# Cross-attention of a two-layer decoder step: sample score rows four a step behind a head's maximum, weight parts behind the samples' part of the output, and the first query chunk finished ahead of the second

## The chip, the cores and the metric

The kernel runs on one core of a Trainium2 chip. The metric is the device time of one execution in microseconds (us). Each engine (TensorE or PE, VectorE or DVE, ScalarE or ACT, GpSimd or POOL, SyncE or SP) works through its own list of instructions in order; semaphores make one wait for another. DMA queues move data between the chip's memory and the on-chip buffers.

## The reference

One inference step of a decoder trunk of two layers, for a prompt of 256 tokens and for 8 samples of one token each. Both use the same weights, d_model is 1024, and all is fp32.

```python
def trunk(x, conv_state, rec_state, mem_k, mem_v):
    for i in range(2):
        x = x + 0.5 * swiglu(rmsnorm(x, norm_ffn1[i]), w_ffn1_gate[i], w_ffn1_up[i], w_ffn1_down[i])
        x = x + mixer_i(rmsnorm(x, norm_mix[i]))          # short conv (i = 0), gated recurrence (i = 1)
        x = x + cross_attn(rmsnorm(x, norm_xattn[i]), mem_k[i], mem_v[i], w_xq[i], w_xo[i])
        x = x + 0.5 * swiglu(rmsnorm(x, norm_ffn2[i]), w_ffn2_gate[i], w_ffn2_up[i], w_ffn2_down[i])
    return rmsnorm(x, norm_final)

def cross_attn(x, mk, mv, w_q, w_o):                       # 4 heads of 256, 256 memory positions
    q = (x @ w_q).reshape(B, T, 4, 256)
    p = softmax(einsum('bthd,bnhd->bhtn', q, mk) / 16)
    return einsum('bhtn,bnhd->bthd', p, mv).reshape(B, T, 1024) @ w_o
```

The prompt's memory keys and values are computed here, from `rmsnorm(mem) @ w_xkv`, and returned. The samples' keys and values come from two caches of (2 layers, 8 samples, 256 positions, 4 heads, 256): 16 MB a layer that have to be read.

## The kernel before

Activations stand transposed: 128 partitions, 8 slices of the model dimension, 264 columns (256 of the prompt, 8 of the samples). An fp32 product is three products in a reduced format (`mm3`): high part of the weights by high part of x, high by low, low by high. The program's names end in h and l for such parts.

**Weights** come in pieces of 512 KB through one stream (class `Weights`). SP issues the transfer into `raw`, ACT makes the high part `wh` (L110), and DVE or POOL makes the low part `wl` (L125), which is `raw` minus `wh`. `raw` has 6 buffers, the parts 5. In attention `W.lo` gives `wl` to POOL; once both pairs of heads are done for the samples, it gives it back to DVE. `W.after["v"]` holds an instruction, and each later `wl` on DVE is ordered behind it.

**The order of work.** TensorE's program is the spine. `flow.tick()` in it steps each "lane" of generators once, and every generator goes on to its next `yield`: so a generator's instructions come to stand between TensorE's products. A scheduler then lists each engine's instructions by their place in the program; `tc.high_priority` moves some forward, and `order(a, b)` says that `a` stands behind `b` on their engine.

**Attention of a layer** (`attention`): four query chunks, one per head. Chunks 0 and 1 share a pass: the first three slices of the one, the first three of the other, then slice by slice in turn (`project`). Chunks 2 and 3 follow. Then, for each head, the memory's keys and values (`do_kv`, tiles `kv`, 8 slices of 6 products). Then the output projection (`pj`).

Lane 1 holds the prompt: after `do_kv(h)` it transposes the keys (`pkt`), multiplies them by the queries (`psc`, L1070), takes the softmax (DVE maximum `mxp` L1057, ACT exponentials `Pp`, DVE reciprocal `zsp` L1060, ACT scale L1062), transposes the weights (`ppt`, L1084; split into `PTh` on ACT and `PTl` on DVE) and multiplies the values (`po`; result split into `oh` on ACT and `ol` on DVE).

Lane 0 holds the samples. Their scores use no TensorE products: the 256 positions of the 8 samples stand as 16 rows of 128 partitions, and DVE multiplies and sums one row an instruction (L1043, tile `junk`, 16 rows a head). `pq` brings a head's queries into that form. The key cache comes in `ring` tiles of 1 MB (8 rows; two a head, called 2a and 2b for head 2 here); there are four ring tiles, and a tile of head 2 can be fetched only once one of head 0 has been used. After a head's rows stand its maximum `mxs` and ACT's exponential. `sample_rest` follows: `SLACK` steps of pause, then the values of heads 0 and 1 (pair 0) and of heads 2 and 3 (pair 1), 64 DVE instructions `acc` a pair (L1153, L1156; the last two write `total`). Value tiles use the same ring. With the first pair goes `combine`, which joins the maxima and sums over the partitions through three small TensorE steps (`pst`, L1112, L1119, L1129); the first reads `mxs` of all heads. Behind each pair `spt` (L1173, TensorE) contracts `total`, and ACT and DVE split it into the samples' columns of `oh` and `ol` (L1180, L1181).

Of the kernel before, what the change touches and what calls it, by code (L numbers as in the profile page):

```python
# [8 lines left out]
F32 = mybir.dt.float32  # L9
# [4 lines left out]
AX = mybir.AxisListType  # L14
# [4 lines left out]
KT = D // P  # L19
T = 256  # L20
NB = 8
NC = T + NB
# [3 lines left out]
XH = 4  # L26
# [12 lines left out]
RING = 4  # L39
HURRY = 40  # L40
STAGGER = 3
SLACK = 5
STEPS = (3, 5, 7, 9, 11, 13)
LAG = 2
DOWN = ((0, 8), (8, 15), (15, 22))
# [199 lines left out]
def trunk_step(ctx: ExitStack, tc: tile.TileContext, ins, consts, outs, stop=None):  # L245
    nc = tc.nc
# [8 lines left out]
    def mm_bank(name):  # L255
        return pmm.tile([P, 512], F32, tag="mm", name=name)

    def aux_bank(name):
        return paux.tile([P, 512], F32, tag="aux", name=name)

    W = Weights(nc, wp)
    flow = Flow(W)
# [22 lines left out]
    xh = cp.tile([P, KT, NC], F32R, name="xh")  # L285
    xl = cp.tile([P, KT, NC], F32R, name="xl")
# [10 lines left out]
    def order(ins, first, reason):  # L297
        info = mybir.DependencyInfo(mybir.DependencyClass.NoSync, mybir.DependencyReason.DATA)
        tc.add_manual_dep(ins.ins, first.name, info, reason=reason)
# [14 lines left out]
    def act(dst, src, func, **kw):  # L314
        in_line(nc.scalar.activation(dst, src, func, **kw))  # L315
# [21 lines left out]
    def mm3(ps, w, rh, rl, first, last, s=slice(None)):  # L337
        wh, wl = w
        nc.tensor.matmul(ps, wh[:, s], rh, start=first, stop=False)  # L339
        nc.tensor.matmul(ps, wh[:, s], rl, start=False, stop=False)  # L340
        return nc.tensor.matmul(ps, wl[:, s], rh, start=False, stop=last).ins  # L341
# [66 lines left out]
            if not self.done:  # L408
                flow.drain(2)

    def project(nch, rh, rl, evac, kt_major=2, need=None, before=None, late_lo=False):
        if not callable(rh):
            rh, rl = (lambda k, t=rh: t[:, k]), (lambda k, t=rl: t[:, k])
        done = 0
        if kt_major:
            ws = [W.get() for _ in range(kt_major)]
            pss = [(c, j, mm_bank(f"pj{c}_{j}")) for c in range(kt_major) for j in range(2)]
            if late_lo:
                for first in (True, False):
                    for c in range(kt_major):  # L420
                        for r in (rh, rl) if first else (rh,):
                            for k in range(KT):
                                w = ws[c](k)[0 if first else 1]
                                for j in range(2):
                                    flow.passed = nc.tensor.matmul(
                                        pss[2 * c + j][2][:, :NC],
                                        w[:, j * P : j * P + P],
                                        r(k),
                                        start=first and k == 0 and r is rh,
                                        stop=not first and k == KT - 1,  # L430
                                    ).ins
                                if k % 4 == 3 and (first or k < KT - 1 or c < kt_major - 1):
                                    flow.tick()
            else:
                order = [(c, k) for c in range(kt_major) for k in range(STAGGER)]
                order += [(c, k) for k in range(STAGGER, KT) for c in range(kt_major)]
                for n, (c, k) in enumerate(order):
                    if before is not None and c == 0:
                        before(k)
                    for j in range(2):  # L440
                        s = slice(j * P, j * P + P)
                        mm3(pss[2 * c + j][2][:, :NC], ws[c](k), rh(k), rl(k), k == 0, k == KT - 1, s)
                    if n % kt_major == kt_major - 1:
                        if k == HK - 1:
                            W.release_first_halves(kt_major)
                        if n < len(order) - 1:
                            flow.tick()
            W.release()
            if need is not None:
                need.ready()  # L450
            with tc.high_priority(offset=HURRY):
                for c, j, ps in pss:
                    evac(c, j, ps[:, :NC])
            flow.tick()
            done = kt_major
        for c in range(done, nch):
            w = W.get()
            for j in range(2):
                ps = mm_bank(f"pj{c}_{j}")
                for k in range(KT):  # L460
                    mm3(ps[:, :NC], w(k), rh(k), rl(k), k == 0, k == KT - 1, slice(j * P, j * P + P))
                    if k == KT // 2 - 1:
                        flow.tick()
                if j == 1:
                    W.release()
                with tc.high_priority(offset=HURRY):
                    evac(c, j, ps[:, :NC])
                flow.tick()
# [342 lines left out]
    def ffn(norm, nxt):  # L811
        with tc.tile_pool(name="ff", bufs=1) as fp:
# [6 lines left out]
            def evac(c, j, ps):  # L819
# [12 lines left out]
                nc.gpsimd.tensor_sub(al[:, blk], a, ah[:, blk].bitcast(F32))  # L832

            project(FB, xh, xl, evac, need=norm, late_lo=norm.first)
            use_set(LNEXP)
            W.lo = ("p", "v", "v")
# [107 lines left out]
    def attention(l, norm, nxt):  # L944
        with tc.tile_pool(name="at", bufs=1) as ap:
# [4 lines left out]
            ol = ap.tile([P, KT, NC], F32R, name="ol")  # L950
            sc = ap.tile([P, XH, NI], F32, name="sc")
            oz = ap.tile([P, XH, NB], F32, name="oz")
            sampled = set()
            mx, zs, rz = (ap.tile([P, XH], F32, name=n) for n in ("mxs", "zss", "rzs"))
            tops = ap.tile([P, P], F32, name="tops")
            nc.gpsimd.memset(tops, 0.0)
# [68 lines left out]
            def spread(t):  # L1025

                return t.unsqueeze(len(t.shape)).broadcast_to(list(t.shape) + [P // NB])

            def sample_scores(h):

                zq = ap.tile([P, 2, P], F32, tag="zq", name="zq", bufs=1)
                nc.scalar.copy(zq.rearrange("p t (b g) -> p t b g", b=NB), spread(qTs[h][:, :, T:]))
                yield
                if h == 0:
                    yield
                pq = aux_bank("pq")
                for dt in range(2):
                    nc.tensor.transpose(pq[:, dt * P : dt * P + P], zq[:, dt], ident)
                yield
                for i in range(NI):  # L1040
                    t = ring.tiles[l, "k", h, i // 8].rearrange("p (i d) -> p i d", d=XD)
                    junk = ap.tile([P, XD], F32, tag="junk", name="junk", bufs=1)
                    nc.vector.tensor_tensor_reduce(  # L1043
                        junk, t[:, i % 8], pq[:, :XD], 1.0, 0.0, ALU.mult, ALU.add, sc[:, h, i : i + 1]
                    )
                    if i % 8 == 7:
                        ring.done((l, "k", h, i // 8))
                    if i % 5 == 4:
                        yield
                nc.vector.reduce_max(mx[:, h : h + 1], sc[:, h], axis=AX.X, negate=True)  # L1050
                act(sc[:, h], sc[:, h], AF.Exp, bias=mx[:, h : h + 1], accum_out=zs[:, h : h + 1])

            def softmax(src, npart, rows, name):
                pr = ap.tile([npart, rows, NMEM], F32, tag=f"P{name}", name=f"P{name}", bufs=1)
                mx = ap.tile([npart, rows], F32, tag=f"mx{name}", name=f"mx{name}", bufs=2)
                zs = ap.tile([npart, rows], F32, tag=f"zs{name}", name=f"zs{name}", bufs=2)
                nc.vector.reduce_max(mx, src, axis=AX.X, negate=True)  # L1057
                for r in range(rows):
                    act(pr[:, r], src[:, r], AF.Exp, bias=mx[:, r : r + 1], accum_out=zs[:, r : r + 1])
                nc.vector.reciprocal(zs, zs)  # L1060
                for r in range(rows):
                    nc.scalar.activation(pr[:, r], pr[:, r], AF.Copy, scale=zs[:, r : r + 1])  # L1062
                return pr
# [76 lines left out]
            def sample_rest():  # L1140

                for _ in range(SLACK):
                    yield
                steps = combine()
                for pair in range(XH // 2):
# [31 lines left out]
                    with tc.high_priority(offset=HURRY):  # L1177
                        ptv = pt[:, : 4 * NB].rearrange("p (t b) -> p t b", b=NB)
                        ohv, olv = (t[:, 4 * pair : 4 * pair + 4, T:] for t in (oh, ol))
                        nc.scalar.copy(ohv, ptv)  # L1180
                        nc.vector.tensor_sub(olv, ptv, ohv.bitcast(F32))  # L1181
                    sampled.add(pair)
                    yield

# [4 lines left out]
                    W.lo = ("v",)  # L1189

            flow.spawn(1, mem_split())
            project(XH, xh, xl, evac_q, need=norm)
            for h in range(XH):
                do_kv(h)
            out_proj(oh, ol, nxt, late=(KT - 2, lambda k: until(k // 4), lambda: flow.drain(1)))
# [490 lines left out]
```

## Time and profile before

| what | value |
|---|---|
| time, median of 3 runs (lowest, highest) | 1282.48 us (1280.98, 1283.21) |
| time of the profiled execution | 1282.15 us |
| its span in the trace | 1280.4 us |
| mean granted TensorE clock | 0.997 |
| TensorE busy | 1258.7 us, 98% of the span |
| DVE / ACT / POOL busy | 66% / 55% / 27% |
| attention of layer 0, with its output projection | about 300 to 419 us |
| attention of layer 1, the same | about 959 to 1075 us |

A row of the timeline gives start and duration in us, engine, line, operation, output and inputs, the count where rows are joined (x8), and in brackets the idle time of the engine before it with what ended it. A row of the waits gives the waiting engine and line, what it waited for, the total in us, the number of times, and the longest. A row of the windows gives a stretch, its length, then busy time (and instructions) of PE, PE's weight loads, DVE, ACT, POOL, the granted clock of TensorE (1.00 is full), the mean share of the DMA engines, and GB/s.

### The profile page before, as it was taken

The numbers are of one execution on the slowest core, as the hardware profiler recorded it, in microseconds if no ns is written. First come the engines' busy times: TensorE is split into PE (matmuls) and PEld (weight loads), VectorE is DVE, ScalarE is ACT, GpSimd is POOL, SyncE is SP. The second block draws the span as 40 slices with busy tenths as digits, with TensorE's granted clock in tenths as the row PEclk, the third lists the DMA queues.
The fourth block names the chain that finished last, engine by engine and source line by source line (L and its number), as shares of the span: only waits on it lengthen the run. The fifth ranks groups of instructions, "written<-read, shape, count | busy, mean of one in ns | idle before, by whom it ended". The sixth has DMA issues, their size and how long they took to land.

```text
span 1280.4 us, 25535 instructions
## 1 busy us (share of the span) xinstructions
PE 1258.7 (98%) x10039; PEld 1230.7 (96%) x10039; DVE 842.4 (66%) x1625; ACT 703.4 (55%) x1167; POOL 346.9 (27%) x272
## 2 busy tenths in 40 slices
PE   8999999999999999999999999999999999999996
PEld 8999999999789999999999999999999789999996
DVE  7655567758777655546655535887887787766454
ACT  6455544446655645544555544656566666766542
POOL 2211231214864211132111132000016862112220
PEclk9999999999999999999999999999999999999999
DMA  8795556655899666556666556653545997997550
GB/s 274 246 305 177 167 180 190 187 160 178 295 395 318 193 176 189 172 168 191 193 173 191 171 171 190 193 171 122 189 151 172 385 384 248 287 324 227 162 165 35
DMA packets 269898, 270.96 MB, mean 212 GB/s; under 512 B 8777, under 2 KB 259721, under 8 KB 269266
## 3 DMA queue, kind: packets, MB, share of 16 engines
q1 hardware_dynamic: 263870, 263.98, 65.4%
q10 hardware_dynamic: 5908, 5.35, 1.2%
q8 instruction: 79, 1.29, 0.4%
q14 instruction: 41, 0.34, 0.1%
HBM read 259.19 MB, written 10.10 MB: 210 GB/s over the span
## 4 chain that ended last, share of the span: by engine, by line
PE 91%; DVE 3%; ACT 2%; DMA 2%; POOL 1%; issue 1%; SPq 0%; DVEq 0%; POOLq 0%; ACTq 0%
PE pj L340 20%; PE pj L339 20%; PE pj L341 20%; PE dn L339 7%; PE dn L341 7%; PE dn L340 7%; PE kv L987 2%; PE kv L988 2%; PE kv L989 2%; ACT wh L110 1%; DVE wl L125 1%; PE pl L1333 1%; PE psc L1070 1%; DMA ring<-in_cache_mem_k_dram 1%; DVE xl L365 1%; DMA raw<-in_w_xkv_dram 1%
## 5 line engine op out<-in xcount | busy, mean ns | idle before, releaser
L125 DVE TENSOR_TENSOR wl<-raw,wh 128x1024 fp32r<-128x1024 f32 (+1 forms) x334 | 411.7, 1238 | 240.0 <-ACT wh L110 224.2
L339 PE MATMUL pj<-xh,wh 128*128 128x264 f32 x1952 | 557.8, 286 | 0.3 <-DVE g L824 0.3
L340 PE MATMUL pj<-xl,wh 128*128 128x264 f32 x1952 | 553.4, 284 | 0.0
L341 PE MATMUL pj<-xh,wl 128*128 128x264 f32 x1952 | 553.0, 283 | 0.0
L110 ACT CAST wh<-raw 128x1024 fp32r<-128x1024 f32 (+1 forms) x406 | 415.5, 1032 | 215.9 <-PE pj L340 107.8
L339 PEld LDWEIGHTS pj<-xh,wh 128*128 128x128 f32 x1952 | 367.7, 188 | 1.9 <-issue 1.4
L340 PEld LDWEIGHTS pj<-xl,wh 128*128 128x128 f32 x1952 | 368.0, 189 | 0.2
L341 PEld LDWEIGHTS pj<-xh,wl 128*128 128x128 f32 x1952 | 366.1, 188 | 0.0
L125 POOL TENSOR_TENSOR wl<-raw,wh 128x1024 fp32r<-128x1024 f32 (+1 forms) x74 | 173.3, 2356 | 127.2 <-ACT wh L110 108.3
L832 POOL TENSOR_TENSOR al<-a,ah 128x264 fp32r<-128x264 f32 x88 | 90.4, 1029 | 411.2 <-ACT ah L831 411.1
L339 PE MATMUL dn<-ah,wh 128*128 128x264 f32 x704 | 200.9, 285 | 0.0
L341 PE MATMUL dn<-ah,wl 128*128 128x264 f32 x704 | 200.0, 284 | 0.0
L340 PE MATMUL dn<-al,wh 128*128 128x264 f32 x704 | 199.4, 283 | 0.0
L341 PEld LDWEIGHTS dn<-ah,wl 128*128 128x128 f32 x704 | 132.7, 188 | 0.0
L339 PEld LDWEIGHTS dn<-ah,wh 128*128 128x128 f32 x704 | 132.4, 188 | 0.2
L340 PEld LDWEIGHTS dn<-al,wh 128*128 128x128 f32 x704 | 132.5, 188 | 0.0
L315 ACT ACTIVATE g<-g 128x264 f32<-128x264 f32 x88 | 36.9, 424 | 76.6 <-DVE g L824 76.6
L831 ACT CAST ah<-a 128x264 fp32r<-128x264 f32 x88 | 36.0, 413 | 68.2 <-DVE a L830 68.1
L360 ACT ACTIVATE xh<-xT,gains 128x264 fp32r<-128x264 f32 x56 | 28.1, 512 | 72.0 <-DVE xT L858 59.1
L1043 DVE CUSTOM_DVE_ANT_0 junk<-ring,pq 128x256 f32<-128x256 f32 x128 | 53.7, 420 | 12.3 <-DMA ring<-in_cache_mem_k_dram 8.6
L378 POOL TENSOR_TENSOR nacc_norm_xattn<-nacc_norm_xattn,nsq 128x264 f32<-128x264 f32 x14 | 13.6, 972 | 174.8 <-ACT nsq L377 174.5
L1156 DVE SCALAR_TENSOR_TENSOR acc<-ring,sc,acc 128x256 f32<-128x256 f32 x112 | 54.5, 487 | 2.7
(327 smaller groups left out, 1538.7 us busy)
## 6 DMA issues: line engine op xcount, KB each, us to landing
raw<-in_w_ffn_gate_dram SPq DMA_DIRECT2D x88, 512.0 KB, 5.8
raw<-in_w_ffn_up_dram SPq DMA_DIRECT2D x88, 512.0 KB, 4.6
raw<-in_w_ffn_down_dram SPq DMA_DIRECT2D x64, 512.0 KB, 4.1
ring<-in_cache_mem_k_dram SPq DMA_DIRECT2D x16, 1024.0 KB, 8.8
raw<-in_w_xkv_dram SPq DMA_DIRECT2D x64, 256.0 KB, 3.6
ring<-in_cache_mem_v_dram SPq DMA_DIRECT2D x16, 1024.0 KB, 9.1
raw<-in_w_rec_in_dram SPq DMA_DIRECT2D x32, 512.0 KB, 4.3
raw<-in_w_ffn_down_dram SPq DMA_DIRECT2D x32, 384.0 KB, 3.0
```

Of the source, the lines that this page charges most:

```text
L110: ins = self.behind(self.hi[i % len(self.hi)], copy(wh[:, :n], self.raw[i][:, :n]))
L125: ins = eng.tensor_sub(wl[:, :n], self.raw.pop(i)[:, :n], wh[:, :n].bitcast(F32))
L315: in_line(nc.scalar.activation(dst, src, func, **kw))
L339: nc.tensor.matmul(ps, wh[:, s], rh, start=first, stop=False)
L340: nc.tensor.matmul(ps, wh[:, s], rl, start=False, stop=False)
L341: return nc.tensor.matmul(ps, wl[:, s], rh, start=False, stop=last).ins
L360: W.pin(nc.scalar.activation(xh[:, k, :n], src, AF.Copy, scale=gcol(self.name, self.layer, k)))
L831: nc.scalar.copy(ah[:, blk], a)
L832: nc.gpsimd.tensor_sub(al[:, blk], a, ah[:, blk].bitcast(F32))
L987: nc.tensor.matmul(pss[nt], mh[:, k, t], wh, start=k == 0, stop=False)
L1043: nc.vector.tensor_tensor_reduce(junk, t[:, i % 8], pq[:, :XD], 1.0, 0.0, ALU.mult, ALU.add, sc[:, h, i : i + 1])
L1156: nc.vector.scalar_tensor_tensor(dst, t[:, i % 4, j], p, sums, op0=ALU.mult, op1=ALU.add)
```

## The change

Five edits, all in attention, in both layers:

1. A score row generator yields after every 4 rows instead of every 5, so a head takes one step more; `SLACK` goes from 5 to 1, so the samples' values begin at the same step.
2. Each score row is ordered behind the latest prompt maximum `mxp` that the program has made before it (`ahead`).
3. `wl` on DVE is ordered behind the samples' `ol`, the last DVE instruction of a pair (`W.after["v"]`).
4. `project` keeps its last product in `flow.passed`, behind which the small products of the samples are ordered.
5. Query chunks 0 and 1 take slices 3 and 4 in turn; then chunk 0 takes its slices 5 to 7 and is evacuated into `qT`, and only then chunk 1 takes its own.

```diff
-SLACK = 5
+SLACK = 1
...
-    def project(nch, rh, rl, evac, kt_major=2, need=None, before=None, late_lo=False):
+    def project(nch, rh, rl, evac, kt_major=2, need=None, before=None, late_lo=False, split=KT):
...
+        def out(c):
+            if need is not None:
+                need.ready()
+            with tc.high_priority(offset=HURRY):
+                for j in range(2):
+                    evac(c, j, pss[2 * c + j][2][:, :NC])
...
-                order += [(c, k) for k in range(STAGGER, KT) for c in range(kt_major)]
+                order += [(c, k) for k in range(STAGGER, split) for c in range(kt_major)]
+                order += [(c, k) for c in range(kt_major) for k in range(split, KT)]
...
-                        mm3(pss[2 * c + j][2][:, :NC], ws[c](k), rh(k), rl(k), k == 0, k == KT - 1, s)
+                        flow.passed = mm3(
+                            pss[2 * c + j][2][:, :NC], ws[c](k), rh(k), rl(k), k == 0, k == KT - 1, s
+                        )
+                    if split < KT and k == KT - 1:
+                        out(c)
...
-            if need is not None:
-                need.ready()
-            with tc.high_priority(offset=HURRY):
-                for c, j, ps in pss:
-                    evac(c, j, ps[:, :NC])
+            if split == KT:
+                for c in range(kt_major):
+                    out(c)
...
-            sampled = set()
+            sampled, ahead = set(), []
...
-                    nc.vector.tensor_tensor_reduce(
+                    row = nc.vector.tensor_tensor_reduce(
                         junk, t[:, i % 8], pq[:, :XD], 1.0, 0.0, ALU.mult, ALU.add, sc[:, h, i : i + 1]
                     )
+                    if ahead:
+                        order(row, ahead[-1], "heads ahead of rows")
...
-                    if i % 5 == 4:
+                    if i % 4 == 3:
                         yield
...
-                nc.vector.reduce_max(mx, src, axis=AX.X, negate=True)
+                ahead.append(nc.vector.reduce_max(mx, src, axis=AX.X, negate=True).ins)
...
-                        nc.vector.tensor_sub(olv, ptv, ohv.bitcast(F32))
+                        W.after["v"] = nc.vector.tensor_sub(olv, ptv, ohv.bitcast(F32)).ins
...
-            project(XH, xh, xl, evac_q, need=norm)
+            project(XH, xh, xl, evac_q, need=norm, split=5)
```

What it moves is seen at three places of layer 0; layer 1 has the same. The line numbers of attention grow by 10 to 14. The first place is DVE's list between the scores of heads 2 and 3, where the prompt's first maximum `mxp` (head 0) stands. `ring_4221` is tile 3a, the first of head 3; ISA is a score row, with the read of its sum behind it. Before:

```order
L1050 TENSOR_REDUCE mxs<-sc 128x1
L1043 ISA junk,sc<-ring_4221,pq 128x256
L1043 ISA sc 128x1
...
L1043 ISA junk,sc<-ring_4221,pq 128x256
L1043 ISA sc 128x1
L1057 TENSOR_REDUCE mxp<-psc 128x2
```

And now:

```order
L1064 TENSOR_REDUCE mxs<-sc 128x1
L1071 TENSOR_REDUCE mxp<-psc 128x2
L1055 ISA junk,sc<-ring_4221,pq 128x256
L1055 ISA sc 128x1
...
L1074 RECIPROCAL zsp<-zsp 128x2
```

Before, four rows of head 3 stood ahead of `mxp`; now none does, and three rows stand between `mxp` and `zsp`. A little further on DVE, where head 3's rows end and the samples' values begin (`ring_4258` is tile 3b, `ring_4313` and `ring_4321` the first value tile), it was:

```order
L1043 ISA junk,sc<-ring_4258,pq 128x256
L1043 ISA sc 128x1
L1050 TENSOR_REDUCE mxs<-sc 128x1
L1153 TENSOR_SCALAR acc<-ring_4313,sc 128x256 x2
L1156 SCALAR_TENSOR_TENSOR acc<-ring_4313,sc,acc 128x256 x2
L1107 TENSOR_TENSOR ol<-po,oh 128x2x256
```

And now it is:

```order
L1167 TENSOR_SCALAR acc<-ring_4321,sc 128x256
L1055 ISA junk,sc<-ring_4258,pq 128x256
L1055 ISA sc 128x1
...
L1170 SCALAR_TENSOR_TENSOR acc<-ring_4321,sc,acc 128x256
L1064 TENSOR_REDUCE mxs<-sc 128x1
L1170 SCALAR_TENSOR_TENSOR acc<-ring_4321,sc,acc 128x256 x2
L1121 TENSOR_TENSOR ol<-po,oh 128x2x256
```

Five value instructions have come in ahead of `mxs`, among the last four rows, and the first of them stands ahead of those rows. The last place is DVE at the end of the second pair, where the output projection is about to use its result. Before:

```order
L1156 SCALAR_TENSOR_TENSOR total<-ring_4739,sc,acc 128x256 x2
L125 TENSOR_TENSOR wl_5058<-raw_4784,wh_5026 128x1024
L1181 TENSOR_TENSOR ol<-spt,oh 128x4x8
L1091 TENSOR_TENSOR PTl<-ppt,PTh 128x512
L1107 TENSOR_TENSOR ol<-po,oh 128x2x256
```

And now:

```order
L1170 SCALAR_TENSOR_TENSOR total<-ring_4712,sc,acc 128x256 x2
L1074 RECIPROCAL zsp<-zsp 128x2
L1195 TENSOR_TENSOR ol<-spt,oh 128x4x8
L125 TENSOR_TENSOR wl_5058<-raw_4791,wh_5026 128x1024
L1105 TENSOR_TENSOR PTl<-ppt,PTh 128x512
```

The weight part has moved behind `ol`. On the other engines, in words: TensorE's `pq` of head 0 stands 12 products earlier and that of head 3 two slices of `kv` later; the first `pst` one slice earlier; `spt` of pair 0 now stands just at the beginning of `psc` of head 2 instead of one slice of `kv` behind it, and `spt` of pair 1 ahead of `ppt` of head 3 instead of behind it. On SP the transfer of tile 2a stands one pair of weight transfers earlier, that of 2b also.

## Prediction

> **What bounds the kernel now.** I read the page's first part and its chain of waits first, then the waits of TensorE, then the timeline round the two longest of them.
>
> ```profile
> PE 1258.7 (98%) x10039; PEld 1230.7 (96%) x10039; DVE 842.4 (66%) x1625; ACT 703.4 (55%) x1167; POOL 346.9 (27%) x272
> PE 91%; DVE 3%; ACT 2%; DMA 2%; POOL 1%; issue 1%; SPq 0%; DVEq 0%; POOLq 0%; ACTq 0%
> ```
>
> TensorE sets the time, and the change adds and removes no product. So it can only win or lose where TensorE stands still or runs at a lower clock. Its waits in attention are these (engine and line, what it waited for, total us, times, longest):
>
> ```profile
> PE ppt L1084 <- ACT Pp L1062: 3.6, 2, 2.3
> PE pj L340 <- DVE ol L1181: 1.4, 2, 0.7
> PE pj L339 <- ACT oh L1180: 0.5, 2, 0.3
> PE psc L1070 <- ACT KTt L1021: 0.3, 1, 0.3
> ```
>
> Each comes once a layer. The windows round the longest add the clock, the number behind the five engines:
>
> ```profile
> 348.00:350.00 2.00, 0.02 (x1) 0.02 (x1) 1.90 (x10) 2.00 (x7) 0.40 (x1) 0.98 1.09 390
> 350.00:352.00 2.00, 2.00 (x7) 1.59 (x8) 1.86 (x10) 1.84 (x3) 2.00 (x2) 0.50 1.06 406
> 352.00:354.00 2.00, 2.00 (x8) 1.57 (x7) 1.66 (x8) 0.01 (x1) 2.00 (x1) 0.67 1.07 391
> 1006.00:1008.00 2.00, 0.70 (x3) 0.14 (x1) 1.41 (x10) 2.00 (x5) 1.04 (x2) 1.00 1.09 381
> ```
>
> Behind layer 0's wait TensorE runs 2 us at 0.50 and 2 us at 0.67: (1 − 0.50) × 2 + (1 − 0.67) × 2 = 1.66 us more. Layer 1's shorter wait left the clock at 1.00.
>
> **Part 1, the prompt's maximum ahead of head 3's rows (edits 1, 2).** TensorE, ACT and DVE round the wait, layer 0 first:
>
> ```profile
> 341.52 1.99 PE L1070 MATMUL psc<-KTt,qT 128*128 128x256 f32 x8 [0.35 <-ACT KTt L1021]
> 347.26 0.39 PE L989 MATMUL kv<-wh,ml 128*128 128x512 f32 x1
> 349.98 1.30 PE L1084 MATMUL ppt<-ident,Pp 128*128 128x128 f32 x4 [2.33 <-ACT Pp L1062]
> 1007.70 0.94 PE L1084 MATMUL ppt<-ident,Pp 128*128 128x128 f32 x4 [1.30 <-ACT Pp L1062]
> ```
> ```profile
> 342.75 0.17 DVE L1050 TENSOR_REDUCE mxs<-sc 128x1 f32<-128x16 f32 x1
> 345.11 0.42 DVE L1043 CUSTOM_DVE_ANT_0 junk<-ring,pq 128x256 f32<-128x256 f32 x1 [2.19 <-DMA ring<-in_cache_mem_k_dram]
> 346.85 0.69 DVE L1057 TENSOR_REDUCE mxp<-psc 128x2 f32<-128x512 f32 x1
> 353.57 0.17 DVE L1050 TENSOR_REDUCE mxs<-sc 128x1 f32<-128x16 f32 x1
> ```
>
> `psc` ended at 341.52 + 1.99 = 343.51 and DVE was idle, but four rows stood ahead of `mxp` and waited for their ring tile until 345.11. From `mxp` to `ppt` it took 349.98 − 346.85 = 3.13 us. With `mxp` at 343.51, `ppt` could come at 346.64, before the last `kv` product ends (347.65). Three rows still stand between `mxp` and `zsp`, as before, when they began at the end of `mxp`, 346.85 + 0.69 = 347.54. If their tile comes no earlier they begin at 345.11, 2.43 us sooner, and `ppt` comes at 347.55: still in time. So the wait goes: **2.33 + 1.66 = 3.99 us** in layer 0, **1.30** in layer 1. Upper bound: `KTt`'s 0.35 too.
>
> [...]
>
> **What is late next.** DVE's work up to the end of pair 0 is only put in another order, and these are the rows in which it rests, layer 0:
>
> ```profile
> 354.40 1.01 DVE L1153 TENSOR_SCALAR acc<-ring,sc 128x256 f32<-128x256 f32 x2 [0.66 <-DMA ring<-in_cache_mem_v_dram]
> 358.80 0.69 DVE L1107 TENSOR_TENSOR ol<-po,oh 128x512 fp32r<-128x512 f32 x1 [2.34 <-ACT oh L1106]
> 361.23 0.29 DVE L1115 TENSOR_REDUCE pst<-pst 4x8 f32<-4x128 f32 x1 [0.82 <-PE pst L1112]
> 371.13 3.64 DVE L1156 SCALAR_TENSOR_TENSOR acc<-ring,sc,acc 128x256 f32<-128x256 f32 x7
> 376.84 0.87 DVE L1156 SCALAR_TENSOR_TENSOR total<-ring,sc,acc 128x256 f32<-128x256 f32 x2
> 355.00:378.00 23.00, 17.85 (x43) 1.00 1.07 395
> 376.59 1.89 PE L1070 MATMUL psc<-KTt,qT 128*128 128x256 f32 x8
> 379.70 0.51 PE L1173 MATMUL spt<-oz,total 128*128 128x8 f32 x4
> 360.92 0.27 PE L1112 MATMUL pst<-ident,mxs 128*4 128x128 f32 x1
> ```
>
> (The row of windows is DVE's: 23 us, busy 17.85.) Two products of TensorE now stand earlier and read what DVE makes.
>
> *`spt` of pair 0* stands at the beginning of `psc` of head 2, 376.59 in the old time, and 3.99 us less is 372.6. It needs `total`, which ended at 376.84 + 0.87 = 377.71. DVE idled 0.66 us at 354.40 and 23.00 − 17.85 = 5.15 us from 355 to 378, some 0.3 of that behind `total`; TensorE being 4 us earlier, most of it (2.34 and 0.82 were TensorE's lateness) can go. All gone would give 372.0, none 377.7. I take four fifths, about 373.5: TensorE waits 0.9 us. So 3.1 of the 3.99 stay.
>
> *The first `pst`* stands one slice of `kv` earlier (six products, 1.36 us by the kv pace of 0.227): 360.92 − 1.36 − 3.99 = 355.6. It needs head 3's `mxs`, and that now stands behind five value instructions (3.64 / 7 = 0.52 us each, 2.6 in all), the first of which stands ahead of the last four rows (four rows took 346.85 − 345.11 = 1.74 us). `mxs` was at 353.57; the value tile came at 354.40. If DVE is 1.6 us earlier at head 3's rows (343.51 for 345.11) and waits for nothing, `mxs` is at 353.57 − 1.6 + 2.6 = 354.6. If the value tile comes at 351.7 (2.7 us earlier, below) and all of these wait for it, at 351.7 + 2.6 + 1.74 = 356.0. I take 356: 0.4 us of waiting, which is then no longer waited for at `spt`, so nothing more is subtracted. If the tile comes at 354.4 as before, it is 358.7 and TensorE waits 3.1 us: that is the rival below.
>
> Layer 1 has the same places, with a shift of only 1.30:
>
> ```profile
> 1012.66 1.01 DVE L1153 TENSOR_SCALAR acc<-ring,sc 128x256 f32<-128x256 f32 x2 [0.66 <-DMA ring<-in_cache_mem_v_dram]
> 1015.34 0.69 DVE L1107 TENSOR_TENSOR ol<-po,oh 128x512 fp32r<-128x512 f32 x1 [0.61 <-ACT oh L1106]
> 1017.57 0.29 DVE L1115 TENSOR_REDUCE pst<-pst 4x8 f32<-4x128 f32 x1 [0.62 <-PE pst L1112]
> ```
>
> DVE's pauses there, 0.66 + 0.61 + 0.62 = 1.89 us, are longer than the shift; I subtract 0.1: **1.2** stay.
>
> **Part 2, the earlier query chunk (edits 4, 5).** It decides whether the tiles come earlier. SP's list and the DMA's load:
>
> ```profile
> 317.57 9.54 SPq L99 DMA_DIRECT2D raw<-in_w_xkv_dram  x6
> 327.21 0.42 SPq L770 DMA_DIRECT2D ring<-in_cache_mem_k_dram  x1
> 346.25 0.37 SPq L778 DMA_DIRECT2D ring<-in_cache_mem_v_dram  x1
> 320.00:330.00 10.00, 10.00 (x66) 9.13 (x65) 9.11 (x42) 8.09 (x15) 8.95 (x8) 1.00 0.44 140
> 340.00:350.00 10.00, 7.32 (x33) 5.47 (x31) 7.35 (x34) 5.25 (x13) 7.43 (x5) 1.00 1.09 380
> ```
>
> Tile 2a stood behind six weight transfers, two of which held SP until 327.21. It now stands ahead of the last two and needs the first eight rows of head 0, which start some 1.4 us earlier (12 products by 0.12 us). So it can be issued near 321, into a stretch in which the DMA engines are 0.44 busy. From 330 on they are full (1.03 to 1.09), and 1 MB less in that queue is 1.05 MB / 380 GB/s = 2.8 us for whatever is behind it, if SP's issues do not hold it back. No product of TensorE is saved by it: the part costs 0 by itself, and POOL's weight parts and six `ml` swap places without anybody on the path waiting (TensorE has no wait on `wl` or `ml` in the list above). Bounds for tile 3a and the first value tile: 0 to 2.8 us earlier. I take 2.7 for the first, since tile 2a's move is whole, and less is the rival.
>
> **Part 3, the weight part behind `ol` (edit 3).** Layer 0's end:
>
> ```profile
> 400.75 1.01 PE L339 MATMUL pj<-oh,wh 128*128 128x264 f32 x6 [0.27 <-ACT oh L1180]
> 402.46 0.39 PE L340 MATMUL pj<-ol,wh 128*128 128x264 f32 x1 [0.70 <-DVE ol L1181]
> 400.12 2.19 DVE L125 TENSOR_TENSOR wl<-raw,wh 128x1024 fp32r<-128x1024 f32 x1 [0.76 <-ACT wh L110]
> 402.23 0.18 DVE L1181 TENSOR_TENSOR ol<-spt,oh 128x32 fp32r<-128x32 f32 x1
> 399.52 0.96 PE L1173 MATMUL spt<-oz,total 128*128 128x8 f32 x8
> ```
>
> `oh` was there by 400.75, so `ol` can be there by about 400.9, while the six products last to 401.8: the 0.70 goes. The weight part ends 0.2 us later, and the next of the projection's chunks uses it, with 24 products ahead. `spt` standing ahead of `ppt` (four transposes) covers the 0.27. Gain **0.97** a layer (1.4 and 0.5 in the waits are the two layers together). But `spt` is asked for about 0.6 us earlier, at 398.92, and `total` ended near 399.4: up to 0.45 us a layer if DVE gains nothing on TensorE. I take 0.15 each, **−0.3** in all.
>
> **Sum.** 3.1 + 1.2 + 2 × 0.97 − 0.3 = 5.9 us. The profiled execution took 1282.15 us (span 1280.4 and 1.75 us outside it), so 1276.2; the median is 0.33 above that execution, so **1276.5 us**. All gains and no new wait: 3.99 + 0.35 + 1.30 + 1.94 = 7.6, 1274.9.
>
> **Rivals.**
>
> *Half given back.* The tiles come earlier by less than 2 us, or DVE makes up only half its idle time, and TensorE waits 2 to 3 us at the first `pst` or at `spt`, in layer 0, without a lower clock. For it: DVE would have to work almost without a pause for 30 us, and the DMA engines are full. Against it: most of DVE's pauses were TensorE's own lateness. Gain 5.9 − 2.5 = 3.4: 1279.1 (1278 to 1280.3).
>
> *The wait only moves.* `total` and the tiles come when they came, since DMA and not DVE paces them (share 1.09). TensorE loses at `pst` and `spt` what it won at `ppt`; only part 3 stays, less some: 1282.5 − 1.0 = 1281.5. Against it: the first value tile was waited for only 0.66 us, and later value tiles not at all.
>
> *Slower: the first value tile holds `mxs`.* The value instruction among head 3's last rows waits for its tile, and in DVE's order the last four rows, `mxs` and with it the first `pst` wait behind it. SP issued that tile only at 346.25, behind weight transfers that wait for buffers; these may not move. Landing at 354.4 gives `mxs` at 358.7, 3.1 us after TensorE wants it, and by the rows above so long a wait halves the clock too (1.66). Layer 0: 3.99 + 0.97 − 3.1 − 1.66, less 0.4 at `spt`, is −0.2. Layer 1: landing at 1012.66 gives 1012.66 + 2.6 + 1.74 = 1017.0, wanted at 1017.3 − 1.36 − 1.30 = 1014.6; 1.30 + 0.97 − 2.4 − 1.66 − 0.4 = −2.2. Sum: 1282.5 + 2.4 = 1284.9; with `KTt`'s wait doubled to 0.7 in both layers, as `psc` now follows a later `pq`, 1285.6. It decides where the tiles land at their old times: 1 us earlier, the waits are 2.1 and 1.4 us and the clock may stay.
>
> *It does not do what it says*: `mxp` is ahead of the rows in the list, but `psc` itself comes later, since `pq` of head 3 stands directly ahead of it. That only moves two transposes from behind; 0.3 us at most, inside the range.
>
> **How the numbers follow.** Forecast 0.52, half given back 0.23, the wait only moves 0.13, slower 0.12. A difference under 0.2% (2.6 us) cannot be told from none here: faster is below 1279.9, slower above 1285.0. Half given back is faster in about four of five cases. Faster 0.52 + 0.18 = 0.70; same 0.05 + 0.13 + 0.02 (the mildest of slower) = 0.20; slower 0.10. The forecast's own range is 1274.9 to 1278; to leave out no more than two in ten I reach up over the moved wait, to 1281.6, and down to 1274.3.
>
> **What would show it.** Right: no wait of `ppt` on `Pp`, granted clock 1.00 all through the first attention, no wait of `pj` on `ol`, tile 2a issued near 321, `mxs` of head 3 before 356.5. Wrong: a new wait of TensorE on `mxs` or `total` over 1 us, a stretch of clock at 0.50 behind it, or the first value tile landing after 353.

## The result, and the profile after

| what | before | changed |
|---|---|---|
| time, median of 5 runs each (lowest, highest) | 1281.63 us (1280.36, 1283.21) | 1274.49 us (1272.57, 1274.97) |
| ratio, 95% interval | | 0.9943 (0.9930 to 0.9957) |
| profiled execution, its span | 1282.15, 1280.4 us | 1274.37, 1272.5 us |
| first residual add behind attention, layer 0 | 409.0 us | 403.9 us |
| the same, layer 1 | 1065.3 us | 1057.4 us |

The change made the kernel 7.1 us faster, 0.57%. The forecast was 1276.5 (1274.3 to 1281.6). A second measurement gave 0.9933 (0.9921 to 0.9945).

Waits of TensorE in the changed kernel; of attention these are the only ones left of 0.15 us or more:

```profile
PE pst L1143 <- DVE zss L1140: 0.3, 2, 0.2
PE ppt L1098 <- ACT Pp L1076: 0.2, 1, 0.2
```

The waits on `Pp` of head 0, on `KTt`, on `ol` and on `oh` are gone. The timeline of TensorE, DVE and SP round the old wait in layer 0:

```profile
346.90 0.60 PE L1098 MATMUL ppt<-ident,Pp 128*128 128x128 f32 x4
354.96 0.27 PE L1126 MATMUL pst<-ident,mxs 128*4 128x128 f32 x1
373.00 0.51 PE L1187 MATMUL spt<-oz,total 128*128 128x8 f32 x4
...
342.98 0.69 DVE L1071 TENSOR_REDUCE mxp<-psc 128x2 f32<-128x512 f32 x1 [3.07 <-PE psc L1084]
351.42 0.49 DVE L1167 TENSOR_SCALAR acc<-ring,sc 128x256 f32<-128x256 f32 x1 [0.91 <-DMA ring<-in_cache_mem_v_dram]
354.74 0.17 DVE L1064 TENSOR_REDUCE mxs<-sc 128x1 f32<-128x16 f32 x1
358.26 0.49 DVE L1170 SCALAR_TENSOR_TENSOR acc<-ring,sc,acc 128x256 f32<-128x256 f32 x1 [1.14 <-DMA ring<-in_cache_mem_v_dram]
371.50 0.86 DVE L1170 SCALAR_TENSOR_TENSOR total<-ring,sc,acc 128x256 f32<-128x256 f32 x2
```
```profile
318.98 0.38 SPq L782 DMA_DIRECT2D ring<-in_cache_mem_k_dram  x1
```

`ppt` comes 3.1 us earlier and without a wait, and no window of the attention has a clock below 1.00. `mxp` now waits for `psc` and not for a tile: DVE had been done with head 2 3.07 us before. In layer 0 the first `pst` and `spt` of pair 0 find their operands ready (`mxs` ends at 354.91, `total` at 372.36); in layer 1 the first `pst` waits 0.14 us for `mxs`. Tile 2a went out at 318.98 instead of 327.21, and the first value tile came at 351.42 instead of 354.40.

What was given back lies between the two `po` of heads 0 and 1: the second value tile came at 358.26 and DVE had waited 1.14 us for it, ahead of head 1's `mxp`; `ppt` of head 1 waited 0.17 and `pst` 0.15. The lead over the old program fell there from 4.77 us (`po` of head 0: 354.90 to 350.13) to 3.55 (`po` of head 1: 370.57 to 367.02), more than these waits. In the second measurement's profiled execution this did not happen: TensorE idled 0.08 us in all from 336 to 410 us. A wait's row can show less than the delay: that on `ol` in the kernel before says 0.70 us, where the products' starts say 0.97 (below, at edit 3).

### The profile page after: what moved, and what is told of

The parts are those of the page before. It is cut to its first block, busy times and chain, and to the rows that moved or that the text cites. A ratio compares the mean times of both kernels' runs of the same rounds, so it can differ in the third digit from the quotient of the medians.

```text
span 1272.5 us, 25527 instructions
## 1 busy us (share of the span) xinstructions
PE 1256.3 (99%) x10039; PEld 1230.0 (97%) x10039; DVE 839.4 (66%) x1625; ACT 703.6 (55%) x1167; POOL 346.1 (27%) x272
## 4 chain that ended last, share of the span: by engine, by line
PE 93%; DVE 3%; DMA 2%; ACT 1%; issue 1%; POOL 0%; DVEq 0%; SPq 0%; ACTq 0%; POOLq 0%
PE pj L339 21%; PE pj L340 21%; PE pj L341 20%; PE dn L339 7%; PE dn L341 7%; PE dn L340 7%; DMA ring<-in_cache_mem_v_dram 2%; PE kv L1001 2%; PE kv L1000 2%; PE kv L999 2%; PE pl L1347 1%; PE psc L1084 1%; DVE junk L1055 1%; DVE acc L1170 1%; DVE wl L125 0%
```

## The experiments

**Each edit alone.** Four kernels were made from the one before, with edits 1, 2, 3, and 4 with 5. The first has only the order of rows behind the maximum:

```diff
+                    if ahead:
+                        order(row, ahead[-1], "heads ahead of rows")
...
+                ahead.append(nc.vector.reduce_max(mx, src, axis=AX.X, negate=True).ins)
```

> The kernel before with edit 2 alone (score rows ordered behind the latest prompt maximum). In its list the first maximum still stands behind the same four rows of head 3. If the place of the maximum in DVE's list makes the wait, and edit 2 does not move it, TensorE's wait before the first ppt stays near 2.3 us in layer 0 and 1.3 us in layer 1, and the time stays within 1 us of 1282. Rival: the order acts at run time in another way, as the prediction credited edits 1 and 2 together; then the wait goes and the time falls by 4 to 5 us.

Measured: 1282.06 us, ratio 1.0003 (0.9990 to 1.0016). TensorE still waits for `Pp`, 2.1 us in one layer and 3.4 in both:

```profile
PE ppt L1086 <- ACT Pp L1064: 3.4, 2, 2.1
```

Edit 2 by itself does nothing: the four rows stand ahead of the maximum in the program as well, so there is nothing for the order to move, and every engine's list in its trace is that of the kernel before.

Edit 1 alone is two lines:

```diff
-SLACK = 5
+SLACK = 1
...
-                    if i % 5 == 4:
+                    if i % 4 == 3:
```

> The kernel before with edit 1 alone (four rows a step, SLACK 1). In its list the first maximum stands directly behind head 2's last row, and one row stands between it and its reciprocal; the ring tiles are asked for no earlier. If the place in the list is enough, the wait before ppt and the lower clock behind it go: 3.99 + 1.3 = 5.3 us, near 1276.5. If the tiles have to come earlier as well (the prediction's rival), TensorE waits for the first pst or the first spt of the samples by 2 us or more in layer 0, and the gain is under 3 us.

Measured: 1282.29 us, ratio 0.9998 (0.9988 to 1.0008). The wait before `ppt` did go, and the gain did not come. The new wait is neither at `pst` nor at `spt`; it is at `psc`:

```profile
PE psc L1070 <- ACT KTt L1021: 5.7, 2, 3.9
```
```profile
343.02 1.99 PE L1070 MATMUL psc<-KTt,qT 128*128 128x256 f32 x8 [1.84 <-ACT KTt L1021]
349.20 0.60 PE L1084 MATMUL ppt<-ident,Pp 128*128 128x128 f32 x4
```

ACT's timeline of the same kernel shows why `KTt` was late. (The profiled execution is the slowest of the ten, 1286.62 us, and its clock was lower three times.) ACT also sends the new keys and values to memory, two transfers it issues between `Vn` and `Vh`:

```profile
337.04 0.48 ACT L997 ACTIVATE Vn<-kv,rmem 128x256 f32<-128x256 f32 x1
339.19 0.42 ACTq L1001 DMA_DIRECT2D out_dram<-Kn  x1
340.48 0.40 ACTq L1001 DMA_DIRECT2D out_dram<-Vn  x1
340.92 0.62 ACT L1004 CAST Vh<-Vn 128x512 fp32r<-128x512 f32 x1 [3.40 <-DMA raw<-in_w_xkv_dram]
342.39 0.58 ACT L1021 COPY KTt<-pkt 128x512 f32<-128x512 f32 x1
```

Here the two issues end at 340.9, 3.4 us behind `Vn`, and all that stands behind them on ACT waits. The kernel before had the same in small, and the changed kernel has nearly none of it. Before and changed, ACT:

```profile
338.98 0.40 ACTq L1001 DMA_DIRECT2D out_dram<-Vn  x1
339.42 0.62 ACT L1004 CAST Vh<-Vn 128x512 fp32r<-128x512 f32 x1 [2.10 <-DMA ring<-in_cache_mem_k_dram]
```
```profile
337.52 0.43 ACTq L1013 DMA_DIRECT2D out_dram<-Vn  x1
337.99 0.62 ACT L1016 CAST Vh<-Vn 128x512 fp32r<-128x512 f32 x1 [0.65 <-ACT Vn L1009]
```

What ended the wait is in the brackets: the landing of a transfer that SP had issued. In the kernel before it was tile 2b's, issued at 329.80 and landed 9.10 us later, at 338.90, 0.08 us ahead of the issue for `Vn` (338.98). Here the issue for `Kn` (339.19) came as tile 2b did (DVE waited 0.54 us for it and began its first row on it at 339.24), and the bracket behind the issue for `Vn` (340.48) names a weight transfer. In the changed kernel the bracket names no transfer, and no score row waits for its tile. That ACT's issues wait for such landings is the author's reading of these times; why they do was not shown.

So the maximum's place in DVE's list was not enough. With the tiles at their old times, ACT's transfers wait as well, and the stall only moves up from `ppt` to `psc`.

Edits 4 and 5 alone (edit 4 was not run apart from edit 5):

```diff
-                order += [(c, k) for k in range(STAGGER, KT) for c in range(kt_major)]
+                order += [(c, k) for k in range(STAGGER, split) for c in range(kt_major)]
+                order += [(c, k) for c in range(kt_major) for k in range(split, KT)]
...
-            project(XH, xh, xl, evac_q, need=norm)
+            project(XH, xh, xl, evac_q, need=norm, split=5)
```

> The kernel before with edits 4 and 5 alone (query chunk 0 finished first). In its list the first maximum now stands behind seven rows of head 3 instead of four, but the ring tile of these rows is asked for earlier. If the place in the list is what counts, the wait before ppt grows by 3 rows, 1.3 us, to 3.6 us in layer 0, and the time rises by 2 us or more. If the arrival of the tile is what counts (345.1 before, about 342 now), the wait shrinks to about 1 us, the clock stays up, and the time falls by about 3 us in layer 0.

Measured: 1274.98 us, ratio 0.9950 (0.9936 to 0.9965): nearly the whole gain, with the maximum in a worse place than before. Its DVE and TensorE rows:

```profile
338.60 0.17 DVE L1062 TENSOR_REDUCE mxs<-sc 128x1 f32<-128x16 f32 x1
343.16 0.69 DVE L1069 TENSOR_REDUCE mxp<-psc 128x2 f32<-128x512 f32 x1 [1.23 <-PE psc L1082]
346.83 0.60 PE L1096 MATMUL ppt<-ident,Pp 128*128 128x128 f32 x4
```

Head 2's rows are done at 338.77 instead of 342.92. The seven rows of head 3 find their tile and are finished before `psc` is: the maximum waits for `psc` (1.23 us), and `ppt` waits for nothing. What is left is the weight part ahead of `ol`, 1.26 us in layer 0, none in layer 1.

Edit 3 alone:

```diff
-                        nc.vector.tensor_sub(olv, ptv, ohv.bitcast(F32))
+                        W.after["v"] = nc.vector.tensor_sub(olv, ptv, ohv.bitcast(F32)).ins
```

> The kernel before with edit 3 alone (weight part on DVE behind the samples' ol). Theory: the wait of pj on ol, 0.70 us a layer, goes, and that on oh, 0.27 us, stays since spt still stands behind ppt: 1.4 us in all, near 1280.5. Rival: the weight part, 2 us long and now later, is itself waited for further on: no gain.

Measured: 1278.78 us, ratio 0.9977 (0.9968 to 0.9986), which is 2.9 us (1.8 to 4.1), more than the 1.4 us of its wait rows. The wait on `ol` went, that on `oh` stayed (0.28 us in each layer). A part of the difference is the rows': in the kernel before, the product that waited for `ol` started 0.99 us after the one ahead of it and the next 0.23 us later, where they else start 0.12 us apart, so this wait cost 0.97 us a layer, 1.9 in both. The rest is likely the clock, which falls behind this wait too in some executions; the profiled execution of the kernel with edit 2 alone, whose lists are those of the kernel before, has it in both layers, here in layer 0 (windows as above, the clock behind the five engines):

```profile
400.00:402.00 2.00, 1.28 (x8) 1.07 (x9) 2.00 (x3) 0.00 (x0) 0.49 (x1) 0.97 1.03 329
402.00:404.00 2.00, 2.00 (x11) 2.00 (x11) 0.27 (x1) 0.00 (x0) 0.00 (x0) 0.50 1.11 310
404.00:406.00 2.00, 2.00 (x14) 2.00 (x14) 0.00 (x0) 0.05 (x1) 0.00 (x0) 0.68 1.06 266
```

There the stop was 0.28 + 0.71 us, and it cost (1 − 0.97) × 2 + (1 − 0.50) × 2 + (1 − 0.68) × 2 = 1.70 us more.

**Is it the transfer, or the earlier rows?** Edit 5 moves products, starts head 0's rows 1.7 us earlier (316.44 to 314.76), and lets tile 2a out earlier. Two kernels part these. One has edits 4 and 5, and holds tile 2a's transfer (`got`) behind the pair of weight transfers (`W.sent` is the last one) where it stood before; TensorE, ACT and POOL keep their lists, and DVE all but the order of three rows late in layer 1's output projection.

```diff
-                    if i % 8 == 7:
+                    if i % 8 == 7 and (h or i > 7):
                         ring.done((l, "k", h, i // 8))
+                    if h == 0 and i == 15:
+                        ring.done((l, "k", 0, 0))
...
+                if (h, hf) == (2, 0):
+                    order(got, W.sent, "late tile")
```

> The kernel before with edits 4 and 5 (1274.98 us by itself), and tile 2a's transfer held behind one pair of weight transfers, where it stood before; TensorE, DVE, ACT and POOL keep the lists of that kernel. If the earlier issue of tile 2a is what edit 5 brought, the tiles of head 3 come late again, the first maximum stands behind seven rows that wait, ppt waits 2 to 3.5 us in layer 0 with the lower clock, and the time goes back to 1280 or more. If the earlier start of head 0's rows or the other order of products brought it, the time stays near 1275.

Measured: 1281.42 us, ratio 0.9993 (0.9985 to 1.0002). One transfer, in both layers, takes back nearly the whole 7 us, though head 0's rows start as early as with edit 5 (314.76). SP's, TensorE's and DVE's rows:

```profile
326.61 1.04 SPq L782 DMA_DIRECT2D ring<-in_cache_mem_k_dram  x2
342.63 1.99 PE L1086 MATMUL psc<-KTt,qT 128*128 128x256 f32 x8 [1.25 <-ACT KTt L1035]
349.71 0.95 PE L1100 MATMUL ppt<-ident,Pp 128*128 128x128 f32 x4 [1.18 <-ACT Pp L1078]
1007.58 0.95 PE L1100 MATMUL ppt<-ident,Pp 128*128 128x128 f32 x4 [2.40 <-ACT Pp L1078]
348.14 0.42 DVE L1057 CUSTOM_DVE_ANT_0 junk<-ring,pq 128x256 f32<-128x256 f32 x1 [2.37 <-DMA ring<-in_cache_mem_k_dram]
```

The maximum was not what waited in layer 0, against the expectation: it started at 344.75, as `psc` ended (344.62). The rows that wait for their tile are those between it and its reciprocal, which ACT needs before `ppt`. `KTt` was late behind ACT's exponential for head 2, which waited 1.42 us for `mxs`.

The other kernel is the one before, with nothing changed but that weight transfers of the layer stand behind tile 2a's on SP from there on, which moves tile 2a ahead of one pair:

```diff
+            if self.front is not None:
+                self.order(ins, self.front, "early tile")
...
+                if (h, hf) == (2, 0):
+                    W.front = got.ins
```

> The kernel before, with nothing changed but that tile 2a's transfer stands ahead of one pair of weight transfers on SP instead of behind it; all other engines keep their lists. If the issue of tile 2a alone makes the difference, the transfer goes out near 320.5 us instead of 327.2, the wait of ppt falls below 0.5 us in layer 0 and the clock stays up: 3 to 5 us gained, near 1278. If SP or the weight stream turns the gain into a later weight transfer, TensorE waits elsewhere and the time stays near 1282.

Measured: 1278.18 us, ratio 0.9968 (0.9955 to 0.9981). The transfer went out at 320.76. `ppt` waits no more, though the four rows still stand ahead of the maximum. The end of the attention waits as before, and `po` waits once, 0.34 us. SP's row, and the longest of TensorE's waits in attention:

```profile
320.76 0.42 SPq L773 DMA_DIRECT2D ring<-in_cache_mem_k_dram  x1
```
```profile
PE pj L343 <- DVE ol L1186: 1.4, 2, 0.7
```

So the earlier issue of one transfer of 1 MB a layer is worth 3.8 us by itself, and without it edit 5 brings nothing that can be told from none. The other 3 us of edit 5 were not taken apart: it lets tile 2a out 1.8 us sooner still, and `spt` of pair 1 stands ahead of `ppt`. This transfer (3.8 us) and edit 3 (2.9 us), each alone, add up to 6.7 of the 7.1 us, but no kernel holds just the two.

**Each edit taken back from the changed kernel.**

> The changed kernel without the earlier query chunk (edit 5). The first maximum stands ahead of all rows of head 3, with one row between it and its reciprocal; tile 2a is asked for near 327 again. If the tiles' arrival is needed for the gain, as the prediction says, TensorE waits at the first pst or spt, or at ppt for the reciprocal behind the late row: 2 us or more lost against 1274.5. If the place in the list is enough, within 1 us of it.

```diff
-            project(XH, xh, xl, evac_q, need=norm, split=5)
+            project(XH, xh, xl, evac_q, need=norm)
```

Without edit 5 (edit 4 stays): 1278.00 us, 0.9973 (0.9963 to 0.9984), which is what edit 3 alone gives (0.9977). The place where it loses was not expected: `psc` waits for `KTt`, 2.04 us in layer 0, with the same late issues on ACT as in the kernel with edit 1 alone, and the clock fell to 0.50 behind it (0.86, 0.50 and 0.78 in the windows of 2 us from 342 to 348). TensorE's row and ACT's:

```profile
343.09 3.47 PE L1084 MATMUL psc<-KTt,qT 128*128 128x256 f32 x8 [2.04 <-ACT KTt L1033]
340.99 0.62 ACT L1016 CAST Vh<-Vn 128x512 fp32r<-128x512 f32 x1 [3.61 <-DMA raw<-in_w_xkv_dram]
```

> The changed kernel without edit 3. Theory: pj waits for ol again by about 0.7 us a layer: 1.4 us slower, near 1276. Rival: with spt ahead of ppt, ol is early enough anyway: no change.

```diff
-                        W.after["v"] = nc.vector.tensor_sub(olv, ptv, ohv.bitcast(F32)).ins
+                        nc.vector.tensor_sub(olv, ptv, ohv.bitcast(F32))
```

Without edit 3: 1276.66 us, 0.9953 (0.9937 to 0.9970). One wait on `ol` is back, 1.26 us in layer 0, and none in layer 1; `ppt` of head 1 waits 0.68 us there, which this run does not explain.

> The changed kernel without edit 2. In its list the first maximum is again behind four rows of head 3. In the changed kernel DVE was idle for 3.07 us ahead of the maximum, waiting for psc. If the place in the list counts by itself, ppt waits again: four rows of 0.46 us behind psc, 1.9 us, less what slack there is, so 1 to 2 us a layer are lost. If the tile now comes early enough for the four rows to be done while psc runs, nothing is lost: within 1 us of 1274.5.

```diff
-                    if ahead:
-                        order(row, ahead[-1], "heads ahead of rows")
```

Without edit 2: 1277.84 us, 0.9964 (0.9949 to 0.9979). `ppt` of head 0 did not wait, so the second expectation held there. But it is slower for another reason, at `pst` and `ppt` of head 1 (waits of TensorE, then DVE's row):

```profile
PE pst L1131 <- DVE tops L1128: 1.8, 2, 1.3
PE ppt L1096 <- ACT Pp L1074: 1.3, 2, 0.7
```
```profile
357.81 0.49 DVE L1168 SCALAR_TENSOR_TENSOR acc<-ring,sc,acc 128x256 f32<-128x256 f32 x1 [2.28 <-DMA ring<-in_cache_mem_v_dram]
```

With edit 1 and without edit 2, a value instruction that waits 2.28 us for the second value tile stands ahead of the reduction that `pst` needs. Edit 2 mends what edit 1 does here.

> The changed kernel without edit 1 (five rows a step, SLACK 5). The first maximum stands behind seven rows of head 3. If place counts, a wait of 2 us or more before ppt comes back in layer 0 with the lower clock, 1.3 us or more in layer 1: near 1279. If the tile's arrival makes up for it, under 1 us is lost.

```diff
-SLACK = 1
+SLACK = 5
...
-                    if i % 4 == 3:
+                    if i % 5 == 4:
```

Without edit 1: 1272.92 us, 0.9930 (0.9913 to 0.9946). Nothing was lost, though the maximum stands behind seven rows: the tile's arrival makes up for it.

**Are edits 1 and 2 worth anything on top of the others?** The kernel before with edits 3, 4 and 5 (their diffs stand above) ran beside the changed kernel itself.

> Edits 3, 4 and 5 without edits 1 and 2; its lists are those of the changed kernel without edit 1, so it should come out at 1272.9 as that did, 1.5 us below the changed kernel, if edit 1 costs what its waits at ppt of head 1 and pst show. If edit 1 costs nothing, it is no different from the changed kernel.

> The changed kernel itself beside the three others on the same chip: 1274.5, if edit 1 costs about 1.5 us; the same as the kernel with edits 3, 4 and 5 if not.

Side by side on one chip: edits 3, 4 and 5 alone 1273.56 us, 0.9930 (0.9918 to 0.9942); the changed kernel 1273.86 us, 0.9933 (0.9921 to 0.9945). They cannot be told apart, so edit 1 does not cost the 1.5 us that was thought possible, and edits 1 and 2 together bring nothing that shows. None of these kernels clearly beats the changed one.

## Why the prediction was right, and where it was not

**The time.** 1276.5 was forecast, 1274.49 measured, inside the range and on the side forecast. The gain was 7.1 us for 5.9.

**The wrong step is part 1 of the sum: whose gain it is.** It booked 2.33 + 1.66 us in layer 0 and 1.30 in layer 1 on edits 1 and 2, since "four rows stood ahead of `mxp` and waited for their ring tile", and it put part 2, the earlier query chunk, at "0 by itself". The row shows two things, a place in a list and a late tile, and either could be put right. Put right alone, the place (edit 1) gave 0.9998, and edit 2, which does not move it, 1.0003; the tile (edits 4 and 5) gave 0.9950, and one transfer moved on SP 0.9968. The prediction saw that the tiles decide whether the gain is kept, and expected the loss at `pst` and `spt`. It overlooked that ACT's transfers of the new keys and values wait in the same stretch, so that without the earlier tile the loss comes before `psc`. The 0.35 us on `KTt` in the waits of before was the trace of it (it comes in layer 0 alone, not once a layer), and was read as a small bound. The prediction's own numbers would have shown what the tile does alone: 2.7 us earlier it is there when head 2's maximum ends (342.92), so the four rows end at 344.66 and `ppt` can come at 344.66 + 3.13 = 347.79, 0.14 us behind the last `kv` product's end instead of 2.33.

**Part 2's chain held where it was forecast.** Tile 2a was put near 321 (318.98), the first value tile at 351.7 (351.42), `mxs` at 356.0 (354.91: the five value instructions and four rows between took 3.3 us for the 4.3 priced). The slower rival, with the value tile at its old time, did not come about.

**What is late next was mis-sized.** 0.9 us were subtracted at `spt` of pair 0, 0.1 in layer 1, and 0.3 at `spt` of pair 1. `total` came at 372.36 for the 373.5 taken (four fifths of the 5.5 us of idle time would have been 373.3), and TensorE asked for it at 373.00: no wait. All 1.3 us taken off did not occur. Without them the sum is 3.99 + 1.30 + 2 × 0.97 = 7.2 us, against 7.1 measured. That the two agree so well is partly luck: 1.2 us of lead were lost in layer 0 at head 1, behind the second value tile, which the prediction had not looked at, while other places gave more than was booked (4.77 us at `po` of head 0 for 3.99).

**Part 3 held.** `ol` and `oh` are waited for no more, and the weight part behind them, 2.02 us now, holds nobody up. But 0.27 of its 0.97 us belongs to edit 5: the wait on `oh` stays with edit 3 alone, and without edit 5 (0.28 us a layer in both). The worth of edit 3 alone, 2.9 us, is above its wait rows, for the reasons given there.

**The clock.** 1.66 us for the lower clock is about right where it comes (1.70 above), but to go by the length of the wait, as the prediction did ("so long a wait halves the clock too", "Layer 1's shorter wait left the clock at 1.00"), does not hold: the kernel with the late tile kept its clock behind 2.40 us, and that with edit 2 alone lost it behind 0.28 + 0.71 us.

## What to carry to other kernels

A wait of one engine on another whose own row says that it waited for a transfer has two cures, and the one to try first is the transfer, which here brought 3.8 us by itself where the place alone brought nothing: find the place in the issuing queue where it stands behind something that holds the queue, and a stretch ahead of it in which the DMA engines are not full (their share was 0.44 here from 320 to 330 us). Take a change of several edits apart in both directions, since here two edits did nothing alone, nothing together on top of the rest, and one of them did harm without the other. And look for every engine that issues transfers, as its other work stands behind the issue: ACT stood still there for 2.10 us in the kernel before and 3.40 with edit 1 alone, until a transfer of SP's had landed.

## What the runs showed of the hardware

The lower clock does not follow from the length of a wait. The kernel with the late tile waited 2.40 us at `ppt` in layer 1, longer than the 2.33 us of before, and kept its clock. Its windows (as above):

```profile
1005.00:1007.00 2.00, 0.18 (x1) 0.00 (x0) 0.95 (x6) 0.00 (x0) 2.00 (x1) 1.00 1.05 398
1007.00:1009.00 2.00, 1.35 (x7) 1.08 (x8) 1.86 (x9) 1.99 (x4) 0.40 (x2) 1.00 1.08 393
1009.00:1011.00 2.00, 2.00 (x10) 1.63 (x10) 1.89 (x8) 1.10 (x4) 2.00 (x1) 1.00 1.06 405
```

And behind the waits on `oh` and `ol` the clock fell in both layers of the kernel with edit 2 alone (0.28 + 0.71 us in layer 0), and in neither of the kernel before (0.27 + 0.70 and 0.27 + 0.71 us). What decides it was not shown. Where it fell, it cost much the same: in the windows of 2 us over the attentions of all these kernels (336 to 410 and 985 to 1065 us) there are eight low stretches, one in the kernel before, three each with edit 2 alone and with edit 1 alone, and one without edit 5. Each goes down to 0.50; seven cost 1.70 to 1.72 us, and the eighth runs on past 1065. For a sum this means that a wait costs its length and, in some of the executions, 1.7 us more. The 18 runs of the kernel before on one chip spread over 6.1 us (1279.64 to 1285.77), the six of the changed kernel there, which has hardly a wait, over 1.2 us (1272.71 to 1273.91). The clock on record goes with it: its mean was 0.997 to 0.998 in the three fastest of the 18 and 0.993 in the slowest, and 0.005 of 1280 us is 6.4 us.

The other is ACT's issue of a transfer. The two issues took ACT from the end of `Vn` 2.1 us before, 3.4 and 3.6 us in the kernels with edit 1 alone and without edit 5, and 0.65 us in the changed one, while the DMA engines' share from 336 to 340 us was 1.07 to 1.09 in the kernels before, changed and with edit 1 alone. The share does not tell them apart; the brackets of `Vh` do: they name the landing of a tile or of a weight transfer in the first three, and none in the changed one.
